# Five of sixteen merge weight units split in a pool of their own beside the mLSTM gates

## The chip, the cores and the metric

The kernel runs on one core of a Trainium2 chip. The time is device microseconds of one launch; what is given for the kernel before is the median of three runs. The program is written in Tile: every tile belongs to a pool, a pool that is opened after another was closed takes over its bytes, and the framework adds the waits that this needs. TensorE (PE) runs in the order in which the program is written; the order of the other engines (VectorE = DVE, ScalarE = ACT, GpSimd = POOL, SyncE = SP) is set by the framework's scheduler from the same program. SP and POOL issue the transfers, each in its own order.

## The reference

Two sequences, of 1024 and 2048 tokens of width 1024, each with 16 meta tokens ahead, go through one layer:

```
xn   = rmsnorm(h);  proj = xn @ w_in + b_in
na_q, na_k, na_v, na_z, ml_qk, ml_v, ml_z, ml_o, ml_g, mg = split(proj)
ya = (neighbourhood_attention(na_q, na_k, na_v) * silu(na_z)) @ w_a
yb = (mlstm_both_directions(conv+silu(ml_qk), ml_v, ml_g, ml_o) * silu(ml_z)) @ w_b
ga, gb = split(sigmoid(mg))
out = h + rmsnorm((ga * ya + gb * yb) @ w_out)
```

The mLSTM works in chunks: from the gates `ml_g` it forms `log_sigmoid`, running sums, and weights `w`; per chunk a state `dC = sum(w v k^T)`, chained over the chunks in both directions, and then the outputs.

## The kernel before

**Numbers.** Every fp32 product is made as three products of rounded halves (`mm3`: high by high, high by low, low by high), so each weight must first be split: ACT copies the raw unit, rounded, to the high half and DVE subtracts it for the low half. A split weight is also stored in DRAM (`w`), 128 partitions x 2 halves, so that later passes load the halves directly. PE runs 15928 matmuls.

**Dense and sparse.** The dense work is a list of groups, `PLAN`: (0,0,"m"), (0,0,"nv"), (1,0,"mv"), (1,1024,"mv"), then the groups with "g", then the final groups "f". A group takes 1024 tokens of a sequence (0 = short, 1 = long) and some column blocks of `w_in`; group j=3, (1,1024,"mv"), is the second long chunk, with nine jobs: two of kind "fm" (four units of 128 columns each), six of kind "tm" (`tm_unit`, two half units `t` of up to 264 columns each, tokens on the output partitions, lines 771 to 773), and a last "fm". The sparse work, `STEPS`, is mLSTM 0 (`ml(0)`), attention 0, mLSTM 1, attention 1. `run()` draws a sparse step, adds its hand-set cost, and then draws dense steps until their costs have made up for it. So attention 0 runs beside group j=3, and the gates of the long mLSTM (`ml(1)`) beside the group (1,1024,"ng").

**The stream of weights.** `requests()` writes down once in which order the weights are wanted (`wreq`). `wload` issues the raw loads (line 274, `wraw`, SP queue), `wpump` splits a unit into one of `NBW = 4` buffers `whl` (ACT line 302, DVE line 303) and stores it (line 326, `w<-whl`, SP queue), or loads a unit that was split earlier (line 295, `whl<-w`; "q" units in line 289). `wtake` hands units to the products in that order.

**The merge units.** The final groups need sixteen units more: eight "m" (`w_a`, `w_b`) and eight "o" (`w_out`). Nothing uses them before that; the stream splits them ahead, between the units of the jobs of j=2 and j=3: `requests()` puts one before each of the first three jobs of j=2, and in j=3 none before the first job, one before the second, and two before each "tm" job. Such a unit takes a `whl` buffer until it has been stored. A unit is 512 KB raw and 1 MB split.

**The long mLSTM.** `ml(1)` opens two pools on the right side: `mg1` (kept to its end) and within it `mt1`, in which `ml_gates` makes the gates: `g_t` is loaded, ACT takes the absolute value and the exponential (`g_e`, lines 1304 and 1306), then the logarithm (`g_ln`, line 1310), DVE finishes `g_lf` (lines 1312 to 1316), and PE sums it with a triangle (`sm<-g_lf,tri`, line 1322). When the gates are done `mt1` is closed and `ml1` is opened in its place; its tiles are the value halves `vwh` and `vwl` (lines 1525, 1526), the key halves `kth`, `ktl`, the states `st`, and the gate rows `um`, which SP loads from DRAM (line 1601). Beside all this the dense group goes on with Strassen-like products (lines 967 to 969) whose banks ACT and DVE empty (lines 994, 996, 1000, 687 to 693).

Of the kernel before, what the change touches and what calls it, by code (L numbers as in the profile page):

```python
# [10 lines left out]
F32 = mybir.dt.float32  # L11
F32R = mybir.dt.float32r
I32 = mybir.dt.int32
AF = mybir.ActivationFunctionType
ALU = mybir.AluOpType
# [3 lines left out]
P = 128  # L19
TCARGS = dict(schedule_with_timeline_sim=True)  # L20
D = 1024
KT = D // P
# [35 lines left out]
def _weight_units():  # L58

    return ([("i", x, P) for x in FM_COLS] + [("t", *c, a) for c in TM_COLS for a in range(2)]  # L60
            + [("m", f, P) for f in range(KT)] + [("o", c, a) for c in range(4) for a in range(2)])


def _sw_order(pairs):

    seq = [(pairs[0], "11")]
    for i, p in enumerate(pairs):
        mid = ("22", "s1") if i == 0 else ("s1", "22")
        seq += [(p, o) for o in ("12", "s2", "s3") + mid]
        if i + 1 < len(pairs):  # L70
            seq.append((pairs[i + 1], "11"))
        seq.append((p, "s4"))
    return seq
# [58 lines left out]

NBW = 4
C512, C256 = 0.235, 0.12
A_N, A_D, A_A, A_G, A_S = (1.08, 0.93), 1.63, 1.79, 1.3, (1.15, 0.91)


class K:
# [420 lines left out]
    def wprep(self):  # L559
# [6 lines left out]
        for p in range(6, 14):  # L566
# [7 lines left out]
            for f, ops in ((0, ("11", "12")), (1, ("21", "22")), (1, ("s3", "s1")), (0, ("s2", "s4"))):  # L574
# [17 lines left out]
                if ops[0] == "11":  # L592
                    yield

    def nprep(self):

        nc = self.nc
        unit = {k: j for j, k in enumerate(_weight_units())}
        op = lambda o, a, b, x=ALU.subtract: nc.vector.tensor_tensor(o, a, b, op=x)
        for p in range(6):  # L600
            r0, r1 = [self.bp.tile([P, 2, 512], F32, name="xr", bufs=4) for _ in range(2)]
            for f, r in enumerate((r0, r1)):
                nc.gpsimd.dma_start(r.rearrange("p a c -> p (a c)"), self.i["wu"][unit["i", PAIRS[p][f], P], :, :D])
            for _ in range(2):
                yield
            op(r1[:, 1], r1[:, 0], r1[:, 1], ALU.add)
            op(r1[:, 0], r0[:, 0], r1[:, 0])
            yield
            op(r0[:, 0], r1[:, 1], r0[:, 0])
            op(r0[:, 1], r0[:, 1], r0[:, 0])  # L610
            yield
            for r, ops in ((r1, ("s3", "s1")), (r0, ("s2", "s4"))):
                hi = self.bp.tile([P, 2, 512], F32, name="xr", bufs=4)
                nc.scalar.activation(hi.bitcast(F32R), r, AF.Copy)
                op(r.bitcast(F32R), r, hi)
                for q, o in enumerate(ops):
                    d = self.qd[p, o] = self.dp.tile([P, D], F32, name=f"q{p}{o}")
                    nc.gpsimd.dma_start(d[:, :512], hi[:, q])
                    nc.gpsimd.dma_start(d[:, 512:], r[:, q])
                yield  # L620
# [228 lines left out]
    def requests(self):  # L849

        unit = {k: j for j, k in enumerate(_weight_units())}
        ahead = deque([("m", f, P) for f in range(KT)] + [("o", c, a) for c in range(4) for a in range(2)])
        for j, (s, t0, cols) in enumerate(PLAN):
            if s == "f":
                assert not ahead
                keys = [("m", f, P) for f in range(KT)] + [("o", c, a) for c in range(4) for a in range(2)]
            else:
                keys = []
                if "g" not in cols:
                    for n, (kind, c) in enumerate(self.layout(cols)):  # L860
                        for _ in range(n < 3 if j == 2 else 0 if j < 2 or n == 0 else 2 if kind == "tm" else 1):
                            if ahead:
                                keys.append(ahead.popleft())
                        keys += [("i", x, P) for x in c] if kind == "fm" else [("t", *c, a) for a in range(2)]
                else:
                    assert not ahead
                    pairs = [p for p in range(14) if "ng"[p > 5] in cols]
                    lead = pairs if (s, t0) not in SW else self.lead(j)
                    keys = [("q", (p, f + "1"), (p, f + "2")) for p in lead for f in "12"]
                    pairs = [p for p in pairs if p not in lead]  # L870
                    if pairs:
                        seq = _sw_order(pairs)
                        keys += [("q", *seq[x:x + 2]) for x in range(0, len(seq), 2)]
            for k in keys:
                if k[0] == "q":
                    self.wreq.append((k, None, KT, P))
                    continue
                nk, w = (KT, P) if k[0] in "im" else (4, k[2] if k[0] == "t" else 256)
                self.wreq.append((k, self.i["wu"][unit[k], :, :nk * w], nk, w))
# [549 lines left out]
    def ml(self, s):  # L1429
        tc, nc = self.tc, self.nc  # L1430
        T, self.seq = SEQLEN[s], s
        NB = T // BL
        with tc.tile_pool(name=f"mg{s}", bufs=1, side="right", reuse_waits="tile") as keep:
            with tc.tile_pool(name=f"mt{s}", bufs=1, side="right", reuse_waits="tile") as mp:
                self.tri = mp.tile([P, 2, P], F32, name="tri")
                nc.sync.dma_start(self.tri, self.i["tri"])
                self.trim = keep.tile([P, 2, 1, P], F32, name="trim")
                nc.sync.dma_start(self.trim[:, :, 0, :], self.i["trimask"])
                self.vas = [keep.tile([P, CB, 130], F32, name=f"va{j}") for j in range(2)]
                for va in self.vas:  # L1440
                    nc.gpsimd.memset(va[:, :, 128:129], 1.0)
                    nc.gpsimd.memset(va[:, :, 129:130], 0.0)
                g, self.keep, self.mlp, sts = [], keep, None, {}
                states = self.ml_states(s, 0, g, NB, sts)
                next(states)
                for j, cost in enumerate(self.ml_gates(s, keep, mp, g)):
                    if j == 3:
                        next(states)
                    yield cost
            with tc.tile_pool(name=f"ml{s}", bufs=1, side="right", reuse_waits="tile") as mp:  # L1450
                self.mlp = mp
                norms = deque()

                def step():
                    for x in tuple(norms):
                        if next(x, "end") == "end":
                            norms.remove(x)

                for h in range(4):
                    if h:  # L1460
                        sts = {}
                        states = self.ml_states(s, h, g, NB, sts)
                    else:
                        yield 2 * A_D + 8.5
                    for cost in states:
                        step()
                        yield cost
                    for cost in self.ml_outputs(mp, s, h, g, NB, sts, norms):
                        step()
                        yield cost  # L1470
                while norms:
                    step()
                    step()
                    yield A_A
        self.done.add(("ml", s))
        self.seq = None
# [696 lines left out]
```

## Time and profile before

| | |
|---|---|
| median of 3 runs | 2693.14 us (2692.37 to 2694.61) |
| the profiled execution: its time | 2696.86 us |
| the profiled execution: its span | 2694.8 us |
| mean granted TensorE clock | 0.993 |
| PE busy | 2642.9 us, 98% of the span |
| DVE, ACT, POOL busy | 1942.1 (72%), 1439.8 (53%), 196.0 (7%) |
| bytes moved, mean rate | 805.74 MB, 299 GB/s |

Times in rows are microseconds from the start of the span. In a row of the timeline the first number is the start, the second the duration, and what stands in brackets at the end is how long the engine had been idle before and what released it. "SPq" and "POOLq" mark rows of those engines' issues. The clock is given as a share of full speed. A line number is one of the kernel before unless it is said to be one of the changed kernel; the changed kernel's lines stand one lower down up to the new function, 18 from there to `ml`, and 24 in and behind `ml`.

### The profile page before, as it was taken

What the parts mean: (1) busy time and instruction counts of PE and PEld (TensorE: products, weight loads), DVE (VectorE), ACT (ScalarE), POOL (GpSimd) and SP (SyncE); (2) the same over time, 40 slices, a digit from 0 to 9 for tenths busy, and PEclk for the clock granted to TensorE, in tenths of its full rate; (3) what the DMA queues carried; (4) which work ended last, traced back from release to release, by engine and by line L of the source; (5) the groups of instructions that cost most, each with busy time, mean ns of one, the idle gap of its engine ahead of it and who ended that gap; (6) DMA issues with size and microseconds to landing.
All of it is one profiled execution on the core that took longest, in us unless ns stands there. A gap on an engine that the chain in (4) does not pass through costs nothing.

```text
span 2694.8 us, 47090 instructions
## 1 busy us (share of the span) xinstructions
PE 2642.9 (98%) x15928; PEld 2334.2 (87%) x15928; DVE 1942.1 (72%) x5266; ACT 1439.8 (53%) x3388; POOL 196.0 (7%) x418
## 2 busy tenths in 40 slices
PE   9999999999999899999999999999999999999998
PEld 7998897899988899887888888887889898989888
DVE  5655678788667776646686777767478989898954
ACT  5423556554446554546665666655365666656521
POOL 0111130011301113100000000000000000000000
PEclk9999999999999999999999999999999999999999
DMA  9898988798867997989889998899899898998965
GB/s 367 330 333 336 330 289 316 278 350 303 285 221 255 356 339 275 313 282 279 262 266 336 364 305 265 278 340 341 256 332 306 262 310 275 289 303 263 339 227 203
DMA packets 394881, 805.74 MB, mean 299 GB/s; under 512 B 50608, under 2 KB 173440, under 8 KB 390800
## 3 DMA queue, kind: packets, MB, share of 16 engines
q1 hardware_dynamic: 363088, 702.49, 77.5%
q0 software_dynamic: 31552, 100.25, 10.1%
q8 instruction: 126, 2.06, 0.3%
q14 instruction: 115, 0.94, 0.1%
HBM read 548.96 MB, written 253.60 MB: 298 GB/s over the span
## 4 chain that ended last, share of the span: by engine, by line
PE 86%; DMA 6%; DVE 5%; ACT 1%; issue 1%; SPq 0%; DVEq 0%; ACTq 0%
PE pj L202 10%; PE pj L204 10%; PE pj L203 9%; PE pj L967 7%; PE pj L969 7%; PE pj L968 7%; PE pj L771 4%; PE pj L773 4%; PE pj L772 4%; PE pj L1929 3%; PE pj L1928 3%; PE pj L1930 3%; PE sm L1262 2%; DMA whl<-w 2%; PE tr L1247 2%; DMA wraw<-wu 1%
## 5 line engine op out<-in xcount | busy, mean ns | idle before, releaser
L202 PE MATMUL pj<-xh,whl 128*128 128x512 f32 (+1 forms) x960 | 369.7, 385 | 2.9 <-ACT whl L302 2.3
L204 PE MATMUL pj<-xh,whl 128*128 128x512 f32 (+1 forms) x960 | 361.4, 376 | 0.3 <-DVE whl L303 0.3
L203 PE MATMUL pj<-xl,whl 128*128 128x512 f32 (+1 forms) x960 | 360.3, 375 | 0.1
L771 PE MATMUL pj<-whl,xh 128*128 128x256 f32 (+1 forms) x1152 | 332.1, 288 | 17.3 <-DMA whl<-w 17.2
L773 PE MATMUL pj<-whl,xl 128*128 128x256 f32 (+1 forms) x1152 | 327.7, 284 | 0.0
L772 PE MATMUL pj<-whl,xh 128*128 128x256 f32 (+1 forms) x1152 | 327.3, 284 | 0.0
L771 PEld LDWEIGHTS pj<-whl,xh 128*128 128x128 f32 x1152 | 220.0, 191 | 18.7 <-DMA whl<-w 18.3
L772 PEld LDWEIGHTS pj<-whl,xh 128*128 128x128 f32 x1152 | 219.7, 191 | 0.2
L773 PEld LDWEIGHTS pj<-whl,xl 128*128 128x128 f32 x1152 | 219.6, 191 | 0.0
L1928 PE MATMUL pj<-whl,mh 128*128 128x256 f32 x768 | 218.3, 284 | 0.9 <-DMA whl<-w 0.9
L1929 PE MATMUL pj<-whl,mh 128*128 128x256 f32 x768 | 216.3, 282 | 0.0
L1930 PE MATMUL pj<-whl,mlo 128*128 128x256 f32 x768 | 215.5, 281 | 0.0
L204 PEld LDWEIGHTS pj<-xh,whl 128*128 128x128 f32 x960 | 181.3, 189 | 35.7 <-DVE whl L303 0.5
L202 PEld LDWEIGHTS pj<-xh,whl 128*128 128x128 f32 x960 | 181.3, 189 | 34.7 <-ACT whl L302 3.2
L967 PE MATMUL pj<-xh,whl 128*128 128x512 f32 x512 | 206.9, 404 | 1.7 <-ACT pj L984 1.1
L203 PEld LDWEIGHTS pj<-xl,whl 128*128 128x128 f32 x960 | 181.7, 189 | 30.6 <-issue 1.0
L969 PE MATMUL pj<-xh,whl 128*128 128x512 f32 x512 | 202.0, 394 | 0.0
L968 PE MATMUL pj<-xl,whl 128*128 128x512 f32 x512 | 201.0, 393 | 0.0
L1249 ACT ACTIVATE pts<-tr 96x384 fp32r<-96x384 f32 (+2 forms) x192 | 103.6, 540 | 107.2 <-PE tr L1247 106.7
L1254 DVE TENSOR_TENSOR pts<-tr,pts 96x384 fp32r<-96x384 f32 (+2 forms) x192 | 118.6, 618 | 55.4 <-ACT pts L1249 53.6
L202 PE MATMUL pj<-yh,whl 128*128 128x512 f32 x384 | 154.1, 401 | 0.0
L203 PE MATMUL pj<-yl,whl 128*128 128x512 f32 x384 | 151.5, 394 | 0.7 <-DVE yl L1830 0.7
(370 smaller groups left out, 6865.8 us busy)
## 6 DMA issues: line engine op xcount, KB each, us to landing
whl<-w SPq DMA_DIRECT2D x136, 1024.0 KB
whl<-q SPq DMA_DIRECT2D x112, 512.0 KB
w<-whl SPq DMA_DIRECT2D x36, 1024.0 KB
wraw<-wu SPq DMA_DIRECT2D x48, 512.0 KB
gt<-st SPq DMA_DIRECT2D x96, 256.0 KB
tg<-gt SPq DMA_DIRECT2D x96, 256.0 KB
q<-po POOLq DMA_DIRECT2D x26, 512.0 KB, 6.7
xt<-xt SPq DMA_DIRECT2D x24, 512.0 KB
```

The costliest lines, as they stand in the source:

```text
L202: mm(out, ah, bh, start=start, stop=False)
L203: mm(out, ah, bl, start=False, stop=False)
L204: mm(out, al, bh, start=False, stop=stop)
L771: nc.tensor.matmul(o, xh, wh, start=k == 0, stop=False)
L772: nc.tensor.matmul(o, xh, wl, start=False, stop=False)
L773: nc.tensor.matmul(o, xl, wh, start=False, stop=k == KT - 1)
L967: mm(bank, w[:, 0, k], xh[:, k], start=fresh and k == 0, stop=False, skip_group_check=True)
L968: mm(bank, w[:, 0, k], xl[:, k], start=False, stop=False, skip_group_check=True)
L969: mm(bank, w[:, 1, k], xh[:, k], start=False, stop=k == 3, skip_group_check=True)
L1928: nc.tensor.matmul(o, mh[:, k, xs], wh, start=clear > 0 and k == 0, stop=False)
L1929: nc.tensor.matmul(o, mh[:, k, xs], wl, start=False, stop=False)
L1930: nc.tensor.matmul(o, ml[:, k, xs], wh, start=False, stop=clear < 2 and k == KT - 1)
```

## The change

The list of merge units gets a name, `MERGE`, and its last five (all "o") leave the stream. A new generator, `mprep`, loads each of them on the POOL queue into a tile `mr`, copies it rounded to `mh` on ACT, subtracts in place on DVE and stores both halves on the POOL queue. Both names have two buffers. `ml(1)` opens a pool `ma1` for it inside `mt1`, draws one step of it before each step of the gates, and draws what is left when the gates are done; then `ma1` and `mt1` are closed and `ml1` is opened on their bytes. The eight units that stay for j=3 go one before each of its first eight jobs.

```diff
@@ -132,6 +132,7 @@
 
 NBW = 4
 C512, C256 = 0.235, 0.12
+MERGE = [("m", f, P) for f in range(KT)] + [("o", c, a) for c in range(4) for a in range(2)]
 A_N, A_D, A_A, A_G, A_S = (1.08, 0.93), 1.63, 1.79, 1.3, (1.15, 0.91)
 
 
@@ -592,6 +593,23 @@
                 if ops[0] == "11":
                     yield
 
+    def mprep(self, pool):
+
+        nc = self.nc
+        unit = {k: j for j, k in enumerate(_weight_units())}
+        for key in MERGE[-5:]:
+            r = pool.tile([P, D], F32, name="mr", bufs=2)
+            nc.gpsimd.dma_start(r, self.i["wu"][unit[key], :, :D])
+            yield
+            yield
+            hi = pool.tile([P, D], F32, name="mh", bufs=2)
+            nc.scalar.activation(hi.bitcast(F32R), r, AF.Copy)
+            nc.vector.tensor_tensor(r.bitcast(F32R), r, hi, op=ALU.subtract)
+            d = self.wkept[key] = self.dp.tile([P, 2, D], F32, name=f"w{len(self.wkept)}")
+            for q, x in enumerate((hi, r)):
+                nc.gpsimd.dma_start(d[:, q], x)
+            yield
+
     def nprep(self):
 
         nc = self.nc
@@ -849,18 +867,18 @@
     def requests(self):
 
         unit = {k: j for j, k in enumerate(_weight_units())}
-        ahead = deque([("m", f, P) for f in range(KT)] + [("o", c, a) for c in range(4) for a in range(2)])
+        ahead = deque(MERGE[:-5])
+        self.wseen.update(MERGE[-5:])
         for j, (s, t0, cols) in enumerate(PLAN):
             if s == "f":
                 assert not ahead
-                keys = [("m", f, P) for f in range(KT)] + [("o", c, a) for c in range(4) for a in range(2)]
+                keys = MERGE
             else:
                 keys = []
                 if "g" not in cols:
                     for n, (kind, c) in enumerate(self.layout(cols)):
-                        for _ in range(n < 3 if j == 2 else 0 if j < 2 or n == 0 else 2 if kind == "tm" else 1):
-                            if ahead:
-                                keys.append(ahead.popleft())
+                        if ahead and (j == 2 and n < 3 or j == 3):
+                            keys.append(ahead.popleft())
                         keys += [("i", x, P) for x in c] if kind == "fm" else [("t", *c, a) for a in range(2)]
                 else:
                     assert not ahead
@@ -1443,10 +1461,16 @@
                 g, self.keep, self.mlp, sts = [], keep, None, {}
                 states = self.ml_states(s, 0, g, NB, sts)
                 next(states)
-                for j, cost in enumerate(self.ml_gates(s, keep, mp, g)):
-                    if j == 3:
-                        next(states)
-                    yield cost
+                with tc.tile_pool(name=f"ma{s}", bufs=1, side="right", reuse_waits="tile") as pool:
+                    side = self.mprep(pool) if s else iter(())
+                    for j, cost in enumerate(self.ml_gates(s, keep, mp, g)):
+                        if j == 3:
+                            next(states)
+                        with self.behind():
+                            next(side, None)
+                        yield cost
+                    for _ in side:
+                        pass
             with tc.tile_pool(name=f"ml{s}", bufs=1, side="right", reuse_waits="tile") as mp:
                 self.mlp = mp
                 norms = deque()
```

The first place is **SP, at the first "tm" job of group j=3**. `w_10287` and the like, with lines 326 or 327, are stores of split merge units; `wraw` are raw loads of the next ones; `w_1017` and `w_1069` are the two halves of the job's weight, split in an earlier group; `sz` are stores of results. Before:

```order
L326 DMA w_10287<-whl 256x1x1024
L274 DMA wraw<-wu 128x1024
L707 DMA sz_252<-st 128x512
L295 DMA whl<-w_1017 128x2112
L326 DMA w_10374<-whl 256x1x1024
L274 DMA wraw<-wu 128x1024
L707 DMA sz_253<-st 128x512
L295 DMA whl<-w_1069 128x2112
```

After:

```order
L327 DMA w_10298<-whl 256x1x1024
L275 DMA wraw<-wu 128x1024
L725 DMA sz_252<-st 128x512
L296 DMA whl<-w_1017 128x2112
L296 DMA whl<-w_1069 128x2112
L725 DMA sz_253<-st 128x512
L725 DMA sz_254<-st 128x512
L327 DMA w_10532<-whl 256x1x1024
L275 DMA wraw<-wu 128x1024
L296 DMA whl<-w_1110 128x2112
```

Of the two stores one is gone, and with it one raw load; the load of the first half `w_1017` still stands behind a store, the load of the second half `w_1069` follows it directly.

The second place is **ACT, in the gates of `ml(1)`**, before (`g_e`, `g_u`, `g_ln` are the gates' tiles, `st<-pj` and `st<-st,bfm` empty the dense group's banks, `th` belongs to the mLSTM's convolution, `g_aR` comes after the triangle product):

```order
L1304 ACTIVATE g_e<-g_t 128x68 x2
L1306 ACTIVATE g_e<-g_e 128x136
L1426 ACTIVATE th<-cv 128x256
L1310 ACT_TABLE_LOAD
L1310 ACTIVATE g_ln<-g_u 128x136
L996 ACTIVATE st<-pj 128x512
L693 ACTIVATE st<-st,bfm 128x512
L1332 ACTIVATE g_aR<-sm 68x128 x2
L1421 ACTIVATE cv<-raw,cw 128x256
```

After (`mh<-mr` is the copy of the new units):

```order
L1322 ACTIVATE g_e<-g_t 128x68 x2
L1014 ACTIVATE st<-pj 128x512
L1324 ACTIVATE g_e<-g_e 128x136
L606 ACTIVATE mh<-mr 128x1024 x2
L1328 ACT_TABLE_LOAD
L1328 ACTIVATE g_ln<-g_u 128x136
L711 ACTIVATE st<-st,bfm 128x512
L1439 ACTIVATE cv<-raw,cw 128x256
L1444 ACT_TABLE_LOAD
L1444 ACTIVATE th<-cv 128x256
L1350 ACTIVATE g_aR<-sm 68x128 x2
```

The copies of the first two units, and one emptying of a bank (line 1014, which was line 996), now stand between the absolute values and the logarithm.

The third place is **ACT and SP at the start of `ml1`**. ACT before (`vwh` are the value halves of the first block of keys):

```order
L687 ACTIVATE st<-pj,bfm 128x512
L688 ACTIVATE st<-pj,bfh 128x512
L1525 ACTIVATE vwh<-va_14366,g_wT_14647 128x130
L1525 ACTIVATE vwh<-va_14366,g_wT_14651 128x130
L1525 ACTIVATE vwh<-va_14366,g_wT_14647 128x130
L1525 ACTIVATE vwh<-va_14366,g_wT_14651 128x130
L1525 ACTIVATE vwh<-va_14367,g_wT_14647 128x130
```

After:

```order
L1439 ACTIVATE cv<-raw,cw 128x256
L1024 ACTIVATE pj<-pj 128x512
L1444 ACTIVATE th<-cv 128x256
L606 ACTIVATE mh<-mr 128x1024
L1549 ACTIVATE vwh<-va_14335,g_wT_14651 128x130
L1549 ACTIVATE vwh<-va_14335,g_wT_14655 128x130
L1549 ACTIVATE vwh<-va_14335,g_wT_14651 128x130
L1549 ACTIVATE vwh<-va_14335,g_wT_14655 128x130
L1576 ACTIVATE kth<-tr 128x256
```

The value halves, which stood behind the emptying of two banks, now stand behind the copy of the fifth unit. And SP, before, where the semaphores that an issue waits for stand in brackets (DMAHW: transfers of SP's queue, DMASW: transfers of POOL's queue):

```order
L289 DMA whl<-q5s_12708 128x1024 [waits DMAHW5_49]
L1601 DMA um<-ud_267 128x2x128 [waits DMAHW6_49,DMAHW1_49]
L1601 DMA um<-ud_268 128x2x128 [waits DMAHW7_49,DMAHW2_49]
L1601 DMA um<-ud_267 128x2x128 [waits DMAHW0_49]
L707 DMA nz_152<-st 128x512 [waits DVE_49]
L1601 DMA um<-ud_268 128x2x128
L1482 DMA va_14366<-mv_247 128x2x128 [waits DMAHW3_49,DVE_49]
L1613 DMA tog<-to_257 128x4x128 [waits DMAHW4_49,Pool_49]
L1482 DMA va_14367<-mv_247 128x2x128 [waits DMAHW5_49,DVE_49]
L1614 DMA szg<-sz_252 128x512 [waits DMAHW6_49,PE_49,Pool_49]
```

After:

```order
L1625 DMA um<-ud_267 128x2x128 [waits DMASW5_49,DMASW2_49,DMAHW5_49,DMASW0_49,DVE_49]
L1625 DMA um<-ud_268 128x2x128 [waits DMAHW6_49,DMASW7_49,DMASW1_49]
L1625 DMA um<-ud_267 128x2x128 [waits DMAHW7_49]
L1625 DMA um<-ud_268 128x2x128 [waits DMAHW0_49]
L1506 DMA va_14335<-mv_247 128x2x128 [waits DMAHW1_49,DVE_49]
L1637 DMA tog<-to_257 128x4x128 [waits DMAHW2_49,Pool_49]
L1638 DMA szg<-sz_252 128x512 [waits DMAHW3_49,Pool_49]
L1506 DMA va_14336<-mv_247 128x2x128 [waits DMAHW4_49,DVE_49]
L1506 DMA va_14335<-mv_247 128x2x128 [waits DMAHW5_49,DMAHW1_49,DVE_49]
L290 DMA whl<-q5s_12682 128x1024 [waits DMAHW6_49,PE_49]
```

The first load of a gate row `um` now waits for transfers of POOL's queue too, among them the store of the fifth unit's low half, and the loads of `va` and of the dense weights `whl` stand behind it on SP.

## The prediction

> **What bounds the kernel now.** The page's share of engines comes first, then PE's waits, the windows around the largest of them, and PE's rows there.
>
> ```profile
> PE 2642.9 (98%) x15928; PEld 2334.2 (87%) x15928; DVE 1942.1 (72%) x5266; ACT 1439.8 (53%) x3388; POOL 196.0 (7%) x418
> ```
>
> PE is busy for 98% of the span, so what makes it wait moves the end, and nothing else does. Of 52 us idle the waits name a third in one row (total, times, longest):
>
> ```profile
> engine line waited for: us in total, times, longest us
> PE pj L771 <- DMA whl<-w: 17.2, 3, 8.3
> ```
>
> These are the second halves of "tm" weights in group j=3 that land late. The timeline has the three waits in brackets, and under each I put the matmul with which the run of 0.28 and 0.29 us begins again (the slow ones between take 0.41 to 0.43):
>
> ```profile
> 891.20 0.59 PE L771 MATMUL pj<-whl,xh 128*128 128x264 f32 x1 [8.34 <-DMA whl<-w]
> ...
> 894.99 0.29 PE L772 MATMUL pj<-whl,xh 128*128 128x264 f32 x1
> ...
> 955.93 0.39 PE L771 MATMUL pj<-whl,xh 128*128 128x256 f32 x1 [3.73 <-DMA whl<-w]
> ...
> 959.80 0.28 PE L772 MATMUL pj<-whl,xh 128*128 128x256 f32 x1
> ...
> 1019.85 0.58 PE L771 MATMUL pj<-whl,xh 128*128 128x256 f32 x1 [5.13 <-DMA whl<-w]
> ...
> 1024.69 0.28 PE L771 MATMUL pj<-whl,xh 128*128 128x256 f32 x1
> ```
>
> A wait costs twice: what it lasts, and then a stretch at half clock, as windows of 1 us show (PE busy and its count first, the clock third from the end):
>
> ```profile
> 880.00:900.00 20.00, 11.66 (x79) 11.30 (x78) 13.62 (x29) 9.89 (x18) 0.43 (x1) 0.83 1.03 351
> 893.00:894.00 1.00, 1.00 (x6) 1.00 (x6) 1.00 (x4) 0.00 (x0) 0.00 (x0) 0.50 1.01 406
> 895.00:896.00 1.00, 1.00 (x11) 1.00 (x10) 0.31 (x1) 0.59 (x1) 0.00 (x0) 1.00 0.99 334
> ```
>
> Six matmuls per us against eleven. The slow stretches are 3.79, 3.87 and 4.84 us, 12.5 together; at 6/11 of the pace 5/11 of them are lost, 5.7 us. So the most that this place can give is 17.2 + 5.7 = 22.9 us.
>
> **What the change takes away.** SP shows why the halves are late: stores of split merge units and the loads that follow them.
>
> ```profile
> 869.55 1.04 SPq L326 DMA_DIRECT2D w<-whl  x1
> ...
> 873.78 0.32 SPq L295 DMA_DIRECT2D whl<-w  x1
> ...
> 924.28 0.56 SPq L326 DMA_DIRECT2D w<-whl  x1
> ...
> 945.89 0.58 SPq L295 DMA_DIRECT2D whl<-w  x1
> ```
>
> The half issued at 873.78 arrived at 891.2, 17.4 us later, in a window whose DMA share is 1.03: two units' stores and raw loads stood in the same engines. With one unit per job a job's first half finds a free buffer and only its second follows a store; per job 1.5 MB less moves. For the second and third wait (3.73 and 5.13) that suffices: one store and one raw load less, 1.5 MB at the window's 351 GB/s, are 4.3 us, and the first half's load, no longer tied to a store, goes a job sooner. The first (8.34) I leave in part, since its half still follows a store. Between that load's issue and its landing lay the store of 869.55 (1 MB), a raw load (0.5), the first half (1.05) and the half itself (1.05), 3.6 MB; without the first two 2.1 remain, an estimate of 17.4 x 2.1/3.6 = 10.2 us, so it lands at 884 where PE needs it at 891.2 - 8.34 = 882.9. Some 1.1 us of wait stay, and 5/11 of 3.79 = 1.7 of clock. Gain 22.9 - 2.8 = 20, with ends of 22.9 and 12 (that wait kept whole, 8.3 + 1.7).
>
> **What the change adds: the gates.** The first steps of the five units fall between the links of the gates' chain. ACT's rows of that chain before, then PE's, then DVE's:
>
> ```profile
> 1217.05 0.39 ACT L1304 ACTIVATE g_e<-g_t 128x68 f32<-128x68 f32 x2
> ...
> 1218.14 1.28 ACT L1310 ACT_TABLE_LOAD   x1
> 1219.43 0.32 ACT L1310 ACTIVATE g_ln<-g_u 128x136 f32<-128x136 f32 x1
> 1219.65 0.58 ACT L996 ACTIVATE st<-pj 128x512 f32<-128x512 f32 x1
> ...
> 1218.73 0.40 PE L969 MATMUL pj<-t2h,whl 128*128 128x512 f32 x1
> ...
> 1221.76 0.63 PE L1322 MATMUL sm<-g_lf,tri 128*128 128x68 f32 x4
> ...
> 1219.78 0.30 DVE L1312 TENSOR_TENSOR g_lf<-g_lf,g_ln 128x136 f32<-128x136 f32 x1 [1.06 <-ACT g_ln L1310]
> ...
> 1221.36 0.30 DVE L1316 TENSOR_TENSOR g_lf<-g_lf,g_e 128x136 f32<-128x136 f32 x1
> ```
>
> and the line of the groups for a copy of 128 x 1024 (busy us, mean ns of one), which is what the new line 606 of the changed kernel does:
>
> ```profile
> L302 ACT ACTIVATE whl<-wraw 128x1024 fp32r<-128x1024 f32 x45 | 47.5, 1055 | 61.2 <-PE pj L204 27.8 <-PE pj L773 26.8 <-DMA w<-whl 3.8
> ```
>
> DVE's last link ends at 1221.66 and PE takes the triangle at 1221.76: no slack. Now ACT first empties a bank (line 996 then), whose product ends at 1218.73 + 0.40 = 1219.13: to 1219.7; the exponential 0.3; two copies of 128 x 1024, 1.06 each as in line 302, to 1222.1; table load 1.28 and logarithm 0.32, to 1223.7 instead of 1219.75. PE waits 3.9 us, and 1.7 for the clock as after the first wait above: 5.6.
>
> **The round trips.** Each name has two buffers, so unit 3's load waits until unit 1's low half is stored, and unit 5's for unit 3's. The trace has none of these transfers. The nearest rows are the twelve raw units, of the same size, that line 603 loads on POOL's queue (issue to landing: least, median, most), and stores of 512 KB on that queue (median at the end). With them stand POOL's last row before the gates, the two ACT rows ahead of the third and the fifth copy, and the price of a subtraction:
>
> ```profile
> 1202.48 0.23 POOL L1349 MEMSET g_mp<- 1x68 f32 x2
> ...
> DMA to landing us min/median/max: 7.5/9.9/13.0
> ...
> q<-po POOLq DMA_DIRECT2D x26, 512.0 KB, 6.7
> ...
> 1240.51 0.58 ACT L994 ACTIVATE pj<-pj 128x512 f32<-128x512 f32 x1
> ...
> 1252.57 0.42 ACT L1426 ACTIVATE th<-cv 128x256 f32<-128x256 f32 x1 [0.57 <-DVE cv L1424]
> ...
> L303 DVE TENSOR_TENSOR whl<-wraw,whl 128x1024 fp32r<-128x1024 f32 x45 | 54.6, 1220 | 30.7 <-ACT whl L302 30.7
> ```
>
> POOL is free at 1202.5, so the first two loads land at 1212.4, in time. Unit 1 is split by 1222.1 + 1.2 = 1223.3, stored by 1230.5; unit 3's load lands at 1240.4. Its copy stands on ACT behind the bank of line 994, 1240.51 + 0.58 + 5.6 = 1246.7, ends at 1247.8; low half 1249, stored 1255.7, unit 5's load lands at 1265.6. ACT comes to unit 5's copy behind the `th` row: 1252.99 + 5.6 + two copies = 1260.7, and waits 4.9.
>
> The Trainium skill, "DMA: Bandwidth & Descriptors", section "Anatomy of one DMA — SWDGE (gpsimd) path", fits such a transfer as 2.0 us plus its bytes over 436 KB per us, an estimate of 3.2 us for 512 KB; the trace has 9.9 and 6.7, two and three times that, with other traffic in the engines, and I go by the trace. By the page the sum would be 18 instead of 27.
>
> **What stands behind unit 5.** Two things, as the order of ACT and SP shows (third place of the change): the value halves of the first block, and the loads of gate rows `um`, whose tiles lie on the pool's bytes and so wait for unit 5's store, with the values of the third block behind them on SP.
>
> ```profile
> 1238.15 2.46 ACT L1525 ACTIVATE vwh<-va,g_wT 128x130 fp32r<-128x130 f32 x8
> ...
> 1252.60 0.28 PE L202 MATMUL sm<-vwh,kth 128*128 128x260 f32 x1
> ...
> 1257.70 0.28 PE L202 MATMUL sm<-vwh,kth 128*128 128x260 f32 x1
> ...
> 1209.71 0.43 SPq L1412 DMA_DIRECT2D raw<-mk  x1
> ...
> 1213.54 0.51 ACT L1421 ACTIVATE cv<-raw,cw 128x256 f32<-128x256 f32 x1 [1.96 <-DMA raw<-mk]
> ...
> 1237.83 1.41 SPq L1601 DMA_DIRECT2D um<-ud  x3
> ```
>
> Before, the halves were made at 1238.15, 12 us ahead of PE's need at 1252.60. Now: 1265.6 + 1.06 + 2.46 = 1269.1, against 1258.2 with the gates' lag; PE stands 10.9 us. Unit 5's store: 1266.7 + 1.22 + 0.5 + 6.7 = 1275.1. Then SP issues four `um` (1.9) and the values (0.4), which land 3.8 us later (1209.71 to 1213.54): 1281.2. ACT splits them (1.2, half of the eight), with the emptying of a bank (1.3) and a key copy (0.4) between: 1284 for the second block's product, 26.4 behind 1257.70. Nothing behind gives this back: PE is full. With 1.7 for the clock 28; with stores of 4.6 us, as two of that size took,
>
> ```profile
> q10s<-po POOLq DMA_DIRECT2D x2, 512.0 KB, 4.6
> t01l<-xr POOLq DMA_DIRECT2D x1, 512.0 KB, 10.3
> ```
>
> 24. I take 27. The three lags are one lateness and not added: 5.6 and 10.9 are in it. Ends: loads of 13.0 and stores of 10.3 lengthen store 3, load 5 and store 5 by 3.6, 3.1 and 3.6, to 38; everything at 4.6 lets load 5 land before ACT arrives, and gives 1260.7 + 1.06 + 1.7 + 4.6 + 6.1 + 2.9 = 1277, 19.
>
> **No price.** Five copies (5 x 1.06 us) and five subtractions (5 x 1.22) leave ACT and DVE in group j=3, where the window 880 to 900 has ACT at work for 9.89 and DVE for 13.62 of 20 us: nothing is won by that, since PE waits there for transfers. They return beside the gates, where they are priced above as far as PE waits for them; units 2 and 4 go with 1 and 3 and lie under the waits of those. Raw and split bytes are the same, in two stores of 512 KB instead of one of 1 MB, and on POOL's queue, which had nothing else to issue there.
>
> **The sum.** 27 - 20 = +7 us. The profiled execution took 2696.86 us, a span of 2694.8 and 2.1 around it, so 2703.9; the median of the runs is 3.7 lower, 2693.14 + 7 = 2700.
>
> **Rivals.**
> *The "tm" jobs gain little.* The DMA share there is already 1.03; if loads that go sooner only queue behind others, the 8.34 wait and part of the rest stay, and 10 is gained: +17, 2710. For it: 17.4 us for one load. Against: a seventh of the group's weight traffic is gone. 0.17.
> *Short round trips.* All transfers at 4.6 us: cost 19, net -1, 2692, and by the page's price -2, 2691. For it: the 4.6 row. Against: the nearest loads, same size and queue, never took less than 7.5. 0.20.
> *The other side: the states are not held at all.* If unit 5's store has landed by 1257.70 + 5.6 - 2.9 - 3.8 - 2.3 = 1254, SP and ACT are in time and only the gates' 5.6 to 8 remain: -12, 2681. From unit 1's store at 1230.5 that leaves 23.8 us for two loads, two splits (4.6) and two stores: it decides at 4.8 us a transfer, and only if ACT is also free at once, where the bank of line 994 holds it to 1246.7. 0.08.
> *A longer chain*, transfers near 13.0 and 10.3: cost 38, +18, 2711. 0.05.
>
> **How the numbers follow.** My forecast (cost 22 to 32, gain 17 to 22.9; -1 to +15) has 0.50. About 0.2%, 5.4 us, is what a measurement of this kernel can tell from no change; of the 0.50 I put 0.13 within it. Faster: 0.08, and 0.03 of the short round trips with the full gain. Same: 0.13 + 0.17. Slower: 0.37 + 0.17 + 0.05. The range goes from the short round trips with the full gain, 19 - 22.9 = -4, 2689, to a cost of 33 with a gain of 10, 2716; beyond lie the other side and part of the longest chains.
>
> **What would show it.** Right: the waits of "tm" jobs at `whl<-w` shrink to about a microsecond; PE waits some 4 us at the triangle product near 1200; ACT waits for `mr` before the fifth copy and PE for `vwh` near 1240 (the whole is 20 earlier by then); the first `um` issue waits for a store of POOL's queue, and the second block's product is some 27 us later against the gates' start. Wrong: a wait of 8 us left at the first "tm" job; `mr` landing 4 us after issue; `um` issued before 1235; or PE waits in a place not named here.

## The result and the profile after

The changed kernel takes 2708.02 us (median of 4 runs, 2705.45 to 2709.49) beside 2693.27 for the kernel before; the ratio of the two is 1.0046, interval 1.0034 to 1.0057. That is slower by 12.4 us, between 9 and 15.4. The profiled execution took 2709.49 us, with a span of 2707.7 and a mean clock of 0.992.

PE's share on the page, which answers to the first line of the prediction:

```profile
PE 2646.3 (98%) x15928; PEld 2334.6 (86%) x15928; DVE 1942.7 (72%) x5266; ACT 1439.0 (53%) x3388; POOL 203.7 (8%) x433
```

PE is busy 3.4 us longer for the same 15928 matmuls (its mean clock is 0.992 against 0.993), and idle 61.4 us where it was 51.9. The groups of the changed kernel show the products that had waited 17.3 us in group j=3 (busy and mean ns, then the idle time before them):

```profile
L789 PE MATMUL pj<-whl,xh 128*128 128x256 f32 (+1 forms) x1152 | 330.7, 287 | 0.0
```

Nothing is left of that wait. What PE waits for instead (us in total, times, longest):

```profile
PE sm L203 <- ACT kth L1576: 19.1, 4, 9.8
...
PE sm L1233 <- DVE yg L1295: 5.0, 5, 1.9
PE sm L1340 <- issue: 4.0, 1, 4.0
PE pj L203 <- DMA whl<-w: 3.8, 2, 3.6
```

`kth` are the key halves, which ACT makes right behind the value halves `vwh`; `yg` is a result of attention. The rows of PE at those places, in order of time:

```profile
790.69 0.47 PE L203 MATMUL pj<-xh,whl 128*128 128x512 f32 x1 [3.60 <-DMA whl<-w]
...
889.40 0.37 PE L1233 MATMUL sm<-kd,stk 128*128 128x288 f32 x1 [1.91 <-DVE yg L1295]
...
1214.32 0.89 PE L1340 MATMUL sm<-g_lf,tri 128*128 128x68 f32 x4 [4.02 <-issue]
...
1255.25 0.58 PE L203 MATMUL sm<-vwh,kth 128*128 128x260 f32 x1 [9.81 <-ACT kth L1576]
...
1268.67 0.58 PE L203 MATMUL sm<-vwh,kth 128*128 128x260 f32 x1 [5.99 <-ACT kth L1576]
```

PE's order is the same in both kernels, so the same product can be looked up in both traces (one execution of each). The difference of its start is how far the changed kernel is behind at that point:

| the product stands | before, us | after, us | after less before |
|---|---|---|---|
| in the first job of j=3, ahead of 790.69 | 784.57 | 785.54 | +1.0 |
| behind that wait | 790.76 | 797.12 | +6.4 |
| ahead of the first tm job | 879.95 | 886.29 | +6.3 |
| in the first tm job | 902.76 | 902.50 | -0.3 |
| behind the place of the second wait | 992.86 | 987.07 | -5.8 |
| behind the place of the third | 1025.86 | 1013.29 | -12.6 |
| ahead of the triangle product | 1220.36 | 1208.74 | -11.6 |
| behind it | 1243.42 | 1236.09 | -7.3 |
| behind the first block of states | 1256.09 | 1260.91 | +4.8 |
| behind the second | 1262.09 | 1275.14 | +13.0 |
| the span's end | 2694.8 | 2707.7 | +12.9 |

All but 1.0 us of the change happens between 785 and 1275 us; behind that the distance stays between 12.9 and 13.8 us. The tm jobs give 18.9 us, the gates and the first two blocks take 24.7, and the first job of group j=3 takes 5.4. Another 1.0 is lost between the tm jobs and the gates.

How the 24.7 come about is seen on ACT, POOL and SP of the changed kernel. ACT first:

```profile
1208.00 0.57 ACT L1014 ACTIVATE st<-pj 128x512 f32<-128x512 f32 x1
...
1208.68 1.99 ACT L606 ACTIVATE mh<-mr 128x1024 fp32r<-128x1024 f32 x2
1210.69 1.28 ACT L1328 ACT_TABLE_LOAD   x1
1211.98 0.32 ACT L1328 ACTIVATE g_ln<-g_u 128x136 f32<-128x136 f32 x1
...
1252.70 1.06 ACT L606 ACTIVATE mh<-mr 128x1024 fp32r<-128x1024 f32 x1 [7.38 <-DMA mr<-wu]
...
1265.92 1.28 ACT L1549 ACTIVATE vwh<-va,g_wT 128x130 fp32r<-128x130 f32 x4 [7.91 <-DMA va<-mv]
```

The bank, two copies, then the table and the logarithm: the triangle waits 4.02. The fifth copy waits 7.38 for its raw unit, and the first block's values are behind it. The third block's values come at 1265.92, late for another reason, which POOL and SP show:

```profile
1217.17 0.53 POOL L610 DMA_DIRECT2D w<-mr  x1 [5.15 <-DVE mr L607]
1222.88 0.53 POOL L602 DMA_DIRECT2D mr<-wu  x1 [5.18 <-DMA w<-mr]
...
1236.00 0.54 POOL L610 DMA_DIRECT2D w<-mr  x1 [0.71 <-DVE mr L607]
...
1245.39 0.55 POOL L602 DMA_DIRECT2D mr<-wu  x1 [6.15 <-DMA w<-mr]
...
1255.58 0.53 POOL L610 DMA_DIRECT2D w<-mr  x1 [1.00 <-DVE vwl L1550]
```

```profile
1258.63 2.20 SPq L1625 DMA_DIRECT2D um<-ud  x4
1260.94 1.15 SPq L1506 DMA_DIRECT2D va<-mv  x1
```

The third and the fifth load each wait for the store of the unit two before; the gate rows `um` go 3.05 us after the fifth unit's last store was issued, just when it has landed (2.9 us from issue to landing), and the values behind them.

### The profile page after: what moved, and what is told of

It is laid out like the page before. It is cut to its first block, busy times and chain, and to the rows that moved or that the text cites. A ratio compares the mean times of both kernels' runs of the same rounds, so it can differ in the third digit from the quotient of the medians.

```text
span 2707.7 us, 47095 instructions
## 1 busy us (share of the span) xinstructions
PE 2646.3 (98%) x15928; PEld 2334.6 (86%) x15928; DVE 1942.7 (72%) x5266; ACT 1439.0 (53%) x3388; POOL 203.7 (8%) x433
## 4 chain that ended last, share of the span: by engine, by line
PE 84%; DMA 6%; DVE 5%; issue 3%; ACT 2%; SPq 0%; POOL 0%; DVEq 0%; ACTq 0%; POOLq 0%
PE pj L203 9%; PE pj L205 9%; PE pj L204 9%; PE pj L985 7%; PE pj L987 7%; PE pj L986 7%; PE pj L789 5%; PE pj L791 5%; PE pj L790 5%; PE pj L1953 3%; PE pj L1952 3%; PE pj L1954 3%; PE sm L1280 2%; PE tr L1265 2%; DMA whl<-w 1%
```

## The experiments

Each run has its own comparison with the kernel before, on the same chip and at the same time; the changed kernel's 1.0046 is from another comparison. The intervals are about 0.0012 to each side, 3 us, so differences of a few us between kernels are read from the profiles.

**Without the five units.**

```diff
         for key in MERGE[-5:]:
+            self.wkept[key] = self.wkept[MERGE[8]]
+            continue
             r = pool.tile([P, D], F32, name="mr", bufs=2)
```

> Leaves out the whole preparation of the five units (no load, copy, subtraction or store; the final groups load another unit's halves in their place). Theory: from the gates on, the changed kernel falls 23.7 us further behind, all of it from these five units, so without them 2708 - 24 = 2684 us, and neither the triangle product nor the first two blocks of states wait. Rival: a part of the lateness there comes from elsewhere (transfers of the dense group, another order of ACT); then it stays above 2691.

Measured: 2681.73 us, ratio 0.9959 (0.9946 to 0.9971), 0.87% or 23.4 us under the changed kernel's ratio. The waits of its profile:

```profile
PE sm L205 <- DVE ktl L1579: 5.9, 5, 2.6
PE sm L1235 <- DVE yg L1297: 4.1, 5, 1.9
PE pj L203 <- DMA whl<-w: 3.6, 1, 3.6
```

The triangle and the first blocks of states no longer wait; the first job's 3.6 us and attention's waits for `yg` stay. By the same look-up as in the table this run is 13.5 us ahead of the kernel before at the triangle and 14.7 behind the second block, where the changed kernel had fallen back by 24.7. So what is lost from the gates on comes all from the five units, and the other two belong to the new order of the stream.

**Five buffers, no round trips.**

```diff
-            r = pool.tile([P, D], F32, name="mr", bufs=2)
+            r = pool.tile([P, D], F32, name="mr", bufs=5)
...
-            hi = pool.tile([P, D], F32, name="mh", bufs=2)
+            hi = pool.tile([P, D], F32, name="mh", bufs=5)
```

> Five buffers for each name instead of two, so that all five loads are issued at once and no load waits for a store. Theory: of the 23.7 us only the gates' 5.2 stay (two copies ahead of the logarithm), the fifth copy finds its data, and the stores are done before the gate rows are loaded: 2708 - 18 = 2690 us. Rival: what holds the states is five copies and subtractions in ACT's and DVE's order and the reuse of the bytes, not the round trips: less than half of it goes, above 2699.

Measured: 2697.62 us, ratio 1.0015 (1.0006 to 1.0024), 8 us under the changed kernel, where I had said 18. Neither theory has it: the long waits for `vwh` are gone (`kth` keeps 2.7 us of 19.1), since the fifth copy, one of the two in ACT's row at 1231.35, no longer waits until 1252.70, but there is a new one. The load of the convolution's input on SP, ACT's row that waits for it, and PE's:

```profile
1196.87 0.65 SPq L1430 DMA_DIRECT2D raw<-mk  x1
...
1206.45 0.51 ACT L1439 ACTIVATE cv<-raw,cw 128x256 f32<-128x256 f32 x1 [7.88 <-DMA raw<-mk]
...
1210.06 0.80 PE L985 MATMUL pj<-xh,whl 128*128 128x512 f32 x1 [3.95 <-ACT pj L1012]
...
1218.30 1.09 PE L1340 MATMUL sm<-g_lf,tri 128*128 128x68 f32 x4 [3.75 <-issue]
```

The five loads land after 4.6 to 12.3 us, median 8.3:

```profile
DMA to landing us min/median/max: 4.6/8.3/12.3
```

`raw` took 9.6 us from issue to ACT's start, where it had been 5.0 in the changed kernel (issued at 1198.22, used at 1203.22): it was issued while three of the five raw units were still on their way, and in the changed kernel both of the first two had landed by then. ACT keeps its order, so the bank behind `raw` was emptied late and PE waited 3.95. The round trips held the states; taking them away by loading all at once made a wait elsewhere. That the five loads delayed `raw` is inferred from their times, and no run took one of the five away. A fuller machine does not explain it: from 1197 to 1204 us the share of the transfers is 1.02 here and 1.04 in the changed kernel.

**The first job of j=3 without a unit.**

```diff
-                        if ahead and (j == 2 and n < 3 or j == 3):
+                        if ahead and (j == 2 and n < 3 or j == 3 and n):
```

> The eight units of group j=3 go before its jobs 1 to 8 instead of 0 to 7, so its first job has none. Theory: the wait of 3.6 us at the first job (which the kernel before does not have) and its 1.1 us of clock go, and with them perhaps the 2 us that attention is late at 880 to 889: 2703, at least 2701. Rival: the wait comes from the transfers of the next inputs there, not from the unit: it stays, 2708; or the unit before the last job costs what the first one did.

Measured: 2703.65 us, ratio 1.0037 (1.0023 to 1.0051). The wait of 3.60 us at 790.69 is not in its profile any more, and the last job, which now has the unit, does not wait. By the ratio 2.4 us are gained, which the intervals tell neither from the 4.7 expected nor from nothing; what the run shows is that the wait goes with the unit. Attention's first wait (1.91) stays: it does not come from the first job. How that job became late is seen on SP. In the changed kernel a store and a raw load went between the loads of its four units, the last of them at 784.28:

```profile
768.77 0.62 SPq L327 DMA_DIRECT2D w<-whl  x1
769.44 0.85 SPq L275 DMA_DIRECT2D wraw<-wu  x1
...
784.28 0.53 SPq L296 DMA_DIRECT2D whl<-w  x1
```

In the kernel before it was at 780.16, with neither between.

**The same buffers on other bytes.**

```diff
             hi = pool.tile([P, D], F32, name="mh", bufs=2)
+            if key == MERGE[-5]:
+                pad = pool.tile([P, 2560], F32, name="pad")
+                nc.gpsimd.memset(pad[:, :1], 0.0)
```

> A tile of 10 KB per partition that nothing uses, put behind the new units' buffers in their pool: no work is added but one memset, and the buffers come to lie on other bytes. The first gate rows then wait for the fourth unit's store and not for the fifth's, and the second state waits for the fifth unit's high half alone. Theory: the last part of the lateness (7.4 us between the first and the second block of states) is the wait for the fifth unit's last store; it goes, 2701 us, while the 9.8 us wait before the first block stays. Rival: the third block's values come late for another reason (the transfers themselves), no change, 2708.

Measured: 2702.25 us, ratio 1.0029 (1.0017 to 1.0040). SP, POOL and PE:

```profile
1243.64 4.06 SPq L1628 DMA_DIRECT2D um<-ud  x4
...
1252.92 0.53 POOL L613 DMA_DIRECT2D w<-mr  x1 [1.00 <-DVE vwl L1553]
...
1252.60 0.59 PE L203 MATMUL sm<-vwh,kth 128*128 128x260 f32 x1 [9.07 <-ACT kth L1579]
```

The gate rows now go 9 us ahead of the fifth unit's last store, and behind the first block's wait (9.07, kept) no other follows: the 5.99 us are gone. In the lateness against the kernel before there is no step behind the first block (12.1 us for that block, as in the changed kernel, and none after it). So the last 8 us of the lateness were the reuse of bytes: no work, only where a tile lies. By the ratio the gain is 4.6 us; the profiled execution was the fastest of six.

**Two units for each tm job again.**

```diff
-                        if ahead and (j == 2 and n < 3 or j == 3):
+                        for _ in range(n < 3 if j == 2 else 0 if j < 2 or n == 0 else 2 if kind == "tm" else 1):
+                          if ahead:
                             keys.append(ahead.popleft())
```

> The five units stay beside the gates, but the eight units of group j=3 are dealt out as in the kernel before: none for the first job, one for the second, then two for each of the first three tm jobs and one for the fourth. Theory: the waits come from two stores and two raw loads ahead of one job's weights; the first two waits (8.3 and 3.7, with their clock 15.5 us) are back, the third (5.1) is not, and the first job's 4.7 goes: 2708 + 15.5 - 4.7 = 2719 us. Rival: what counts is how many units the group has in all, since the transfers are saturated; with five fewer, the waits stay away even so: 2703.

Measured: 2710.20 us, ratio 1.0057 (1.0043 to 1.0071).

```profile
PE pj L789 <- DMA whl<-w: 11.0, 2, 8.1
```

The first two waits are back (8.1 and 2.8 us; they were 8.34 and 3.73) and the third is not, as expected: what decides is what stands in the queue ahead of a job, not how many units the group has. Two are not always too many: the three waits of the kernel before are in jobs 2, 4 and 6, and jobs 3 and 5 had two units as well and did not wait. The sum was off: 3 us slower than the changed kernel, not 11. I had left out that where a tm job waits, attention does not: its waits for `yg` are 1.9 us in this profile and 5.0 in the changed kernel's. That is 3 of the 8 us; another 2.6 lie ahead of group j=3, where this execution is 1.6 us ahead of the kernel before and the changed kernel's 1.0 behind it, and the rest was not followed up.

**All sixteen in the stream.** These start from the kernel before and change only the number of units ahead of each job.

```diff
-                        for _ in range(n < 3 if j == 2 else 0 if j < 2 or n == 0 else 2 if kind == "tm" else 1):
+                        for _ in range(n < 8 if j == 2 else n > 0 if j == 3 else 0):
```

> The kernel before, with its sixteen units all in the stream, one each: before jobs 0 to 7 of group j=2 and 1 to 8 of j=3; nothing beside the gates. Theory: a tm job bears one unit without a wait, in j=2 as in j=3, so the gain in j=3 (22 to 23 us) comes free: 2694 - 22 = 2672 us. Rival: the transfers of j=2 are already at 0.92 to 1.04 of their time in its tm jobs, and five units more there make PE wait as in j=3: 2680 to 2690.

Measured: 2683.57 us, ratio 0.9958 (0.9945 to 0.9970): faster than the kernel before and the changed one, but the rival was right on j=2, for one job:

```profile
629.41 0.58 PE L771 MATMUL pj<-whl,xh 128*128 128x256 f32 x1 [8.07 <-DMA whl<-w]
```

In the windows from 600 to 640 the share of the transfers is 1.03 and 1.01. So in j=2 one unit ahead of a job can be too many. Four units ahead of the last job of j=2 instead, `(1, 1, 1, 0, 0, 0, 0, 1, 4)[n]`:

> As the one before, but in group j=2 the units go before its first three jobs (one each, as in the kernel before), one before job 7 and four before its last, where the transfers are at 0.48 and 0.25 of their time (720 to 760). Theory: idle transfers take four units without a wait, 2672 us. Rival: four units in a row take all four weight buffers, the job's own four units come after them, and PE waits some 10 us: 2682.

Measured: 2686.72 us, ratio 0.9969 (0.9958 to 0.9981), the rival's case:

```profile
PE pj L202 <- DMA whl<-w: 10.7, 2, 10.5
```

Nine and seven, `j == 2 or j == 3 and 0 < n < 8`:

> All sixteen in the stream, one each before the nine jobs of group j=2 and before jobs 1 to 7 of j=3. Theory: the last job of j=2 has room, the last of j=3 showed 1.8 us of wait with a unit ahead of it: 2 us under the other kernel with one each, 2670. Rival: no difference.

Measured: 2684.19 us, ratio 0.9961 (0.9948 to 0.9973): no difference from one each. The 1.8 us on which I had built are a wait at 8 us, at the kernel's start, which I had taken from the list of waits without looking up its place. Then job 4 of j=2 without a unit, `j == 2 and n != 4 or j == 3 and n > 0`:

> As the kernel with all units in the stream, one each, which waited once more, 8.1 us for the second half of the third tm job of group j=2 (job 4, 629 us): that job gets no unit, and job 8 of j=2 gets one. Theory: the wait is that unit's store and raw load, and goes with its clock: 2684 - 10 = 2674 us. Rival: the transfers of that stretch are full anyway (share 1.03 and 1.01), the unit only moves and another job waits: 2680 or more.

Measured: 2679.90 us, ratio 0.9941 (0.9927 to 0.9954). In place of 8.07 us there is one wait of 1.98 at the job behind (the total of two is 2.7), so the theory holds for most of the wait; by the ratio the time fell by 4.6 us where the theory had 10, and it lies at the edge of the rival's range.

The same with job 5 free, `n != 5`:

> The same, but job 5 of group j=2 is left free instead of job 4, so the unit ahead of the job that waited stays. Theory: the 8.1 us stay, 2684 us. Rival: the wait comes from what had piled up by then, and fewer units later help: 2678.

Measured: 2692.87 us, ratio 0.9992 (0.9983 to 1.0001), slower than either theory. The wait ahead of job 4's second half is there, as the first theory says (6.7 us), and with it one that neither names, in the short mLSTM, where the kernel before waits 1.90:

```profile
704.00 0.58 PE L202 MATMUL sm<-vwh,kth 128*128 128x260 f32 x1 [6.57 <-ACT kth L1552]
```

What made ACT late there was not followed up. The profiled execution was also the fastest of eleven, 5.7 us under the median, so its profile does not account for the whole median. Jobs 3 and 4 free and two units ahead of the last job, `(1, 1, 1, 0, 0, 1, 1, 1, 2)[n]`:

> The same with jobs 3 and 4 of group j=2 free and two units before its last job. Theory: the first job's unit made no wait worth the name (0.5 us), so this differs from the kernel without job 4's unit by 1 us at most, unless two units before the last job hold its own units back as four did (10.5 us): 2674 to 2679.

Measured: 2678.15 us, ratio 0.9935 (0.9922 to 0.9947), within the range, with a wait of 6.66 us at that last job (728.87 us). So the second unit was moved to job 1 of j=3, `(1, 1, 1, 0, 0, 1, 1, 1, 1)[n] if j == 2 else (0, 2, 1, 1, 1, 1, 1, 1, 1)[n] if j == 3 else 0`:

> All sixteen in the stream: in group j=2 one before each job but 3 and 4, in j=3 none before job 0, two before job 1 (four column units, 60 us of products, and the transfers beside it at 0.58 to 0.89 of their time), one before each other. Theory: the 6.7 us wait at the last job of j=2 in the kernel with two units there goes and none comes at job 1 of j=3: 2672 us. Rival: the second unit at job 1 takes one of the four buffers and that job's own units come late: no gain, 2678 to 2680.

Measured: 2674.66 us, ratio 0.9930 (0.9916 to 0.9943), the fastest, though its interval overlaps that of the kernel with two units before the last job of j=2. Its page and the row that is left of the weights' waits:

```profile
PE 2633.1 (99%) x15928; PEld 2325.3 (87%) x15928; DVE 1940.7 (73%) x5266; ACT 1440.0 (54%) x3388; POOL 196.3 (7%) x418
```

```profile
PE pj L202 <- DMA whl<-w: 2.7, 2, 2.2
```

```profile
829.12 0.47 PE L202 MATMUL pj<-xh,whl 128*128 128x512 f32 x1 [2.19 <-DMA whl<-w]
```

The wait at the last job of j=2 is gone; the longer of the two that are left is in job 1 of j=3, where the theory had none and the rival had one. PE idles 36.9 us of a span of 2670.0. No unit is split beside the gates.

## Why the prediction was right, and where its terms were off

The direction, the range and the course of events hold: slower, 2700 foretold and 2708 measured, because the five units take more from the long mLSTM than their absence gives to the tm jobs. Point by point:

- **Gain of the tm jobs, 20.** All three waits went; 18.9 us came of it. I had kept 1.1 us of the first wait, and there was none, so the three places gave 22.4, nearly the 22.9 called the most. What I did not name is what came next: attention's products, which run between those of the tm jobs, then waited themselves (1.91 for `yg` at 889.40; two more, of 0.9 and 1.2, follow up to 1045), and, with their clock, the first two took 3.5 us of the 22.4. Two small figures of the working are off: the lower end of the gain is 22.9 - 10 = 12.9, not 12, and the five units are about a sixth of the group's weight traffic (7.5 of some 44 MB), not a seventh; neither moves the forecast.
- **The step that failed: the first job of j=3.** I read from the diff that the job gets a unit that it had not had, and gave it no price; 5.4 us (3.60 of wait and the clock) were lost there. That is just what lies between 7 and 12.4, which is luck in part: the gain was 1.1 short, 2.0 more were lost ahead of the first job and between the tm jobs and the gates, and the states cost 2.3 less than I had said. The prediction named a wait of PE in a place that it does not name as a sign that it is wrong; this wait and attention's are such. The order of SP in that place would have shown a store and a raw load among the four loads.
- **Gates, 5.6.** The wait was 4.02 against 3.9. At first 5.7 us were lost, and then 1.4 came back, because two waits of 0.80 and 0.31 us, which the kernel before has behind the triangle, are gone: 4.3 from ahead of the chain to behind it.
- **The fifth copy and the first block, 10.9.** ACT waited 7.4 (4.9 foretold), PE 9.81; the first block cost 12.1 with the clock. The second block's part, 9.9 by the working, was 8.2.
- **Their sum, 27.** It was 24.7, and the run without the units gives 23.4. The loads were quicker than their nearest rows and the stores not: from issue to landing the answer for the five loads, then for the ten stores (least, median, most) is

```profile
DMA to landing us min/median/max: 4.5/6.5/7.3
```

```profile
DMA to landing us min/median/max: 2.9/7.9/11.1
```

where I had 9.9 and 6.7. The estimate of 3.2 us from the fit in the Trainium skill, "DMA: Bandwidth & Descriptors", section "Anatomy of one DMA — SWDGE (gpsimd) path", lies under the least of the loads (4.5) and near the least of the stores (2.9); by it the loss would have been 18, and the trace, with 24.7, does not agree.
- **The rivals.** Short round trips: the loads went half the way there, and still the states were held. Little gain in the tm jobs: refuted. The kernel with two units a job shows that what stands ahead of a job is the cause, not the group's total; why jobs 3 and 5 bore two is open.
- **What was argued and is now shown:** that the last stall is reuse of bytes (the padded pool), that all of the loss from the gates on is the five units' (the run without them), that round trips hold the first block (five buffers). That doing without the round trips would be free, as I expected of the five buffers, was wrong.

## What to carry to other kernels

When work is moved out of a stream to relieve one place, price the place where it arrives in links of the chains that run there: an in-order engine that stops for a load holds all that is queued behind it, and a pool that others reuse holds them until its last store has landed. Before moving work to another stage, try to deal it out evenly where it is: sixteen units, nearly all one by one, with two crowded jobs spared, gave 0.7% where moving five lost 0.5%. And of each row that a change of an order touches, ask also what it does at the jobs that had no trouble.

## What the runs showed that was not expected

Five raw units of 512 KB issued within 3 us on POOL's queue landed after a median of 8.3 us, against 6.5 in two and two and one; in the same stretch a small load of SP's queue took 9.6 us until it was used instead of 5.0. And what follows a wait at half clock came on top here too: 9.81 us of wait at the first block cost 12.1, and the window behind it shows six matmuls in a microsecond at a clock of 0.50 (third from the end):

```profile
1257.00:1258.00 1.00, 1.00 (x6) 0.90 (x5) 0.77 (x3) 0.27 (x1) 0.00 (x0) 0.50 0.93 389
```
